# Operand rows of a trunk kernel at multiples of 64 bytes: wider rows of the normalised input and a padded scratch tile

## The chip, the core and the metric

The kernel runs on one core of a Trainium2 chip. The metric is the time of one execution on the device in microseconds, as the median of several runs. A profile of one more execution shows each instruction with its start and its duration, the DMAs, and the clock that TensorE was granted.

## What is computed

A trunk of two layers on 256 tokens with 1024 channels. Each layer is a SwiGLU FFN, a mixer (pooling in layer 0, a gated short convolution in layer 1) and a second FFN. Every sub-layer first normalises its input and modulates it by a shift and a scale, and a gate weighs what it adds; shift, scale and gate come from a vector c by one more product. A last normalisation ends it.

```python
D_MODEL, SEQ, DEPTH, D_FF = 1024, 256, 2, 2816
...
    cond = jax.nn.silu(c)
    for i in range(DEPTH):
        mod = (cond @ ada_w[i] + ada_b[i]).reshape(B, N_SUB, N_MOD, D_MODEL)
        shift, scale, gate = mod[:, :, 0], mod[:, :, 1], mod[:, :, 2]
        h = modulate(rms_norm(x, norm_g[i, 0]), shift[:, 0], scale[:, 0])
        x = x + 0.5 * gate[:, 0, None, :] * swiglu(h, ffn_w_in[i, 0], ffn_w_out[i, 0])
        h = modulate(rms_norm(x, norm_g[i, 1]), shift[:, 1], scale[:, 1])
        ...
        x = x + gate[:, 1, None, :] * y
        h = modulate(rms_norm(x, norm_g[i, 2]), shift[:, 2], scale[:, 2])
        x = x + 0.5 * gate[:, 2, None, :] * swiglu(h, ffn_w_in[i, 1], ffn_w_out[i, 1])
    return rms_norm(x, final_g)
```

## The kernel before

**Two parts for each number.** Most products are done three times over: a float32 number is split into a high part, rounded to the type float32r, and a low part, which is the rest, and the product is hi x hi + lo x hi + hi x lo. The helper mm3 (L135) issues these three matmuls. A matmul has 128x128 weights, loaded by an instruction of its own (LDWEIGHTS), and streams the other operand, 256 tokens wide as a rule; it adds to a bank of the result memory. The tokens stay resident.

**Weights.** They come from memory in units of 1 MB, 128 partitions with 2048 floats each, by DMAs that SyncE issues in the order of use. raw_unit (L191) takes one of four buffers raw. ScalarE copies raw to the high part hi (L230), and VectorE subtracts to get the low part lo (L237); hi and lo have four buffers each. A few units have their parts in gh and gl, the tiles of the FFN's inner values, while these are out of use: there gh and gl are weights, in the first block or two of an input product. The modulation's units go through raw too, with two dot products on VectorE each (L253). One product unit feeds 48 matmuls of 256 columns.

**Inputs.** hh and hl hold the high and the low part of the modulated input, a row of 256 tokens for each of eight blocks k of channels. hh's rows have two floats more, since the first blocks of an FFN begin before the normalisation is known, and carry the two parts of the shift as columns 256 and 257 (shift_columns, L374; mm3s, L380). hf is a float32 version of the same, for the products that use raw weights whole. The input products of the FFNs write banks f00b, f01b, f10b and f11b (and f01a, f10a, f11a for early blocks), in the loop

```python
700  for k in range(KB):
701      for s in range(2):
702          mm3(pab[:, s], (hi[:, k, s], lo[:, k, s]), h_pair(k), k == 0 and s == 0, k == KB - 1)
```

so that one block is 8 rows k with six matmuls each: 48. There are 22 blocks in an FFN: of f00 the first eight go together as the modulation comes in (seven of their eight rows in float32r), of f01, f10 and f11 the first three, two and three are early ones, and the convolution has six later blocks with 72 matmuls each (pcv and pb) behind two early ones (pe). The output products (out_product, L421) write accf and accc with gh and gl as the streamed operand. In the last product (out_last, L474) the roles are changed: gh and gl are the weights, and hi and lo are streamed, in pieces of 512 or 256 columns, to acco. In the pooling mixer, mean (L759) multiplies by mh, a matrix with the averaging windows on its diagonal and zeros elsewhere, as the streamed operand, with gh and gl as weights, to accp.

**Order.** The order on each engine is the order in the code, written out by hand (manual_schedule): low(n) and high(n) say how many units ahead the parts are made.

**Where the tiles lie.** A pool puts its tiles one behind the other, each rounded up to a multiple of 32 bytes in a partition. The pool "one" comes first, then "wk" for scratch, and then "wp" for the weights. In the memory map of the program before:

| tile | bytes in a partition | start, modulo 64 | its rows start at |
|---|---|---|---|
| hf | 8 x 1028 | 32 | 32 + 4k |
| gh, gl | 22 x 1024 | 0 | 0 |
| hh | 8 x 1032 | 0 | 8k |
| hl | 8 x 1024 | 0 | 0 |
| mh | 8256 | 0 | 0 |
| ss (three buffers, the last of wk) | 8, with 32 set aside | 0, 32, 0 | |
| raw, hi, lo (twelve buffers) | 8192 | 32 | 32 |

The weights of one matmul are 128 floats, 512 bytes, so all within a unit have the unit's place. The lines that the text speaks of:

```python
132  def mm(dst, w, m, start, stop):
133      PE.matmul(dst, w, m, start=start, stop=stop, skip_group_check=True)
...
339  hh = one.tile([P, KB, T + 2], F32R, name="hh")
340  hl = one.tile([P, KB, T], F32R, name="hl")
...
382      mm(dst, w[0], hh[:, k], k == 0, False)
383      mm(dst, w[1], hh[:, k], False, False)
384      mm(dst[:, :T], w[0], hl[:, k], False, k == KB - 1)
...
508              s = wk.tile([P, 2], F32, tag="ss", name=f"ss{b}{i}", bufs=3)
```

Of the kernel before, what the change touches and what calls it, by code (L numbers as in the profile page):

```python
# [9 lines left out]
F32 = mybir.dt.float32  # L10
F32R = mybir.dt.float32r
# [14 lines left out]
EDGE = 16  # L26
BAND = P + EDGE
# [15 lines left out]
class Source:  # L43
    """Cuts the weights into [128, 2048] units."""
# [45 lines left out]
def products():  # L90
    """The weight units of the products, in the order of their use. With each, the first of eight
    blocks of the products' inputs that hold its parts, where those are out of use by then; or,
    where it is used whole, whose buffer holds it: that of a high or of a low part."""

    def ffn(layer, f, at, first=False):
        into = [("ffn_first", layer, f, kb) for kb in range(KB)] if first else []
        into += [("ffn_in", layer, f, c) for c in range(0 if into == [] else NFIRST, FC)]
        out = [(("ffn_out", layer, f, u), None) for u in range(FC // 2)]
        return [(c, at[i] if i < len(at) else None) for i, c in enumerate(into)] + out

    conv = []
    for j in range(KB):
        conv.append((("conv_cv", j), 0 if j == 0 else None))
        if j % 2 == 0:
            conv.append((("conv_b", j // 2), 8 if j in (0, 4) else None))
    conv += [(("conv_out", u), None) for u in range(KB // 2)]
    first = ffn(0, 0, WHOLE, True)
    return (
        first[:-TAIL] + [(("pool",), "hi")] + first[-TAIL:]
        + ffn(0, 1, ("hi", "lo", "lo")) + ffn(1, 0, (0, 8)) + conv + ffn(1, 1, (8,))  # L110
    )
# [3 lines left out]
def trunk(ctx: ExitStack, tc: tile.TileContext, calls, consts: bass.AP, c_in: bass.AP,  # L115
# [19 lines left out]
    def mm3(dst, w, m, start, stop):  # L135
        """dst += w.T @ m; w, m: pairs of parts."""
        mm(dst, w[0], m[0], start, False)
        mm(dst, w[1], m[0], False, False)
        mm(dst, w[0], m[1], False, stop)

# [15 lines left out]
    # Token t to token v, for each window: the causal mean, less the token itself. From its place  # L156
    # on the diagonal a token's weights span BAND tokens; those of the first tokens, whose windows
    # are cut, come in with the constants, for a mean over the whole window: cut_means() makes it
    # that over the tokens there are.
# [15 lines left out]
    def table(func):  # L175
        """Has the function's table on the engine before it is needed."""
        tabs.append(wk.tile([P, 1], F32, tag="tab", name=f"tab{len(tabs)}"))
        S.activation(tabs[-1], eps, func)

    # Around the pooling mixer: after which blocks of the FFN's fed input one of its later block's  # L180
    # products goes; how many modulation units go with the blocks of the product before, into the
    # mixer, and with the pairs of blocks after; how far ahead the low parts are then.
# [43 lines left out]
    def high(n, parts=1):  # L226
        """The high parts of the products' next n units."""
        for _, raw, hi, _ in next_of("hi", n):
            for at in spans(parts) if hi else ():
                S.copy(hi[:, at], raw[:, at])  # L230

    def low(n, parts=1):
        """The low parts of the products' next n units."""
        high(n, parts)
        for _, raw, hi, lo in next_of("lo", n):
            for at in spans(parts) if hi else ():
                V.tensor_sub(lo[:, at], raw[:, at], hi[:, at].bitcast(F32))  # L237
# [11 lines left out]
    mods = {}  # L249

    def dot(out, w, init):
        """out = init + sum over w * cond; w becomes w * cond."""
        V.tensor_tensor_reduce(w, w, cond, 1.0, init, ALU.mult, ALU.add, out)  # L253

    def mod_dots(layer, sub, mod, w, lo):
        """Blocks lo... of one modulation vector, with what its use adds to it."""
        key, n = (layer, sub, mod), w.shape[1]
        if key not in mods:
            mods[key] = one.tile([P, KB], F32, name=f"mod{layer}{sub}{mod}")
        b = ada_col(layer, sub, mod) + lo  # L260
        for i in range(n):
            dot(mods[key][:, lo + i : lo + i + 1], w[:, i], cst[:, b + i : b + i + 1])
        mod_finish(key, lo, n)
# [24 lines left out]
    def spread(keys, lo, hi, later=0):  # L288
        """Spreads modulation vectors, but for the last parts, over the slots lo...hi of the
        stream of products to come."""  # L290
        ada_todo.extend((*k, q) for k in keys for q in range(4))
        slots.clear()
        n = len(ada_todo) - later
        for i in range(n):
            at = lo + (i * (hi - lo)) // n
            slots[at] = slots.get(at, 0) + 1
# [31 lines left out]
    def rstd_by_token(name):  # L328
        """With the tokens on the partitions: [128, 2]."""
        m = bank(f"ms{name}")  # L330
        for b in range(2):
            PE.matmul(m[:, 0, b : b + 1], sqs["a"][:, b * P : (b + 1) * P], ones[:, 0:1], start=True, stop=True)
        r = wk.tile([P, 2], F32, tag="rt", name=f"rt{name}", bufs=2)
        S.activation(r, m[:, 0, :2], AF.Sqrt, bias=eps)
        q = wk.tile([P, 2], F32, tag="rt", name=f"rq{name}", bufs=2)
        V.reciprocal(q, r)
        return q

    hh = one.tile([P, KB, T + 2], F32R, name="hh")
    hl = one.tile([P, KB, T], F32R, name="hl")  # L340

    def modulated(layer, sub, k, rstd, to):
        """x * rstd * g * (1 + scale) + shift: its high part, or all of it, and what makes the low
        one."""
        scale, shift = (mods[layer, sub, m][:, k : k + 1] for m in (SCALE, SHIFT))
        t = wk.tile([P, T], F32, tag="t", name=f"t{layer}{sub}{k}", bufs=4)
        V.scalar_tensor_tensor(t, x[:, k], scale, rstd, ALU.mult, ALU.mult)
        S.activation(to[:, k, :T], t, AF.Identity, bias=shift)
        return lambda: V.scalar_tensor_tensor(
            hl[:, k], t, shift, hh[:, k, :T].bitcast(F32), ALU.add, ALU.subtract  # L350
        )
# [13 lines left out]
    def scaled(layer, sub, k, to):  # L365
        """x * g * (1 + scale): what modulated() gives, before rstd and the shift."""
        sc = mods[layer, sub, SCALE][:, k : k + 1]
        S.activation(to[:, k, :T], x[:, k], AF.Copy, scale=sc)
# [5 lines left out]
    def shift_columns(layer, sub, ks=slice(0, KB)):  # L374
        """The shift's two parts beside scaled(), so that the product carries them too."""
# [4 lines left out]
    def mm3s(dst, w, k):  # L380
        """dst += w.T @ [scaled | shift's parts]"""
        mm(dst, w[0], hh[:, k], k == 0, False)
        mm(dst, w[1], hh[:, k], False, False)
        mm(dst[:, :T], w[0], hl[:, k], False, k == KB - 1)

    def unscaled(acc, rstd, name, split=True):
        """The product with the modulated input, in two parts: acc * rstd and the shift's."""
# [33 lines left out]
    def out_product(kind, n, layer, sub, name, after, first_slot, ahead, ready, between=lambda b: None, before=lambda u: None, whole=False):  # L421
        """x += gate * (z @ w), z: n blocks of parts, w: n // 2 units."""
# [39 lines left out]
    def by_token(a, b):  # L462
        """Of the residual and of its gate: channels 32 a..., for tokens 32 b...: tokens on the
        partitions."""
# [9 lines left out]
    def out_last(n, ahead):  # L474
# [24 lines left out]
        for b in range(2):  # L499
            mean, late = eps, []  # L500
            for i, (lo, hi) in enumerate(PIECES[b]):
# [6 lines left out]
                s = wk.tile([P, 2], F32, tag="ss", name=f"ss{b}{i}", bufs=3)  # L508
# [61 lines left out]
    def ffn_start(rstd, name):  # L570
        """The first blocks of the first FFN: all of them at once, as the modulation comes in."""
# [52 lines left out]
    def ffn_early(layer, f, sub, name, groups):  # L624
        """The first blocks of an FFN, begun before rstd is known."""
# [20 lines left out]
    def ffn_fed(layer, f, sub, name, feed, n, ahead):  # L646
        """The same where the input, used whole, comes two blocks at a time: the n-th block fills
        the time between."""
# [83 lines left out]
    def pool_shift():  # L732
        """The shift's product with the pooling mixer's weights, the same for each token."""
# [12 lines left out]
    def pool_layer(after, each):  # L746
# [12 lines left out]
        def mean(acc, g, z, at, first, last):  # L759
            """acc += the means, less the token itself, of the tokens' z."""  # L760
# [158 lines left out]
def blocks(a):  # L919
    """[..., 1024] to [128, ... * 8]: the channel within its block first."""  # L920
# [4 lines left out]
def edge():  # L925
    """For the first tokens: token t to token v, with the weight of a whole window, less the token
    itself as often as its own window holds it; and whole windows over their own."""
# [39 lines left out]
```

## Time and profile before

| | |
|---|---|
| median of three runs | 900.67 us (900.6 to 901.98) |
| span of the profiled execution, first to last instruction | 899.1 us |
| median less span | 1.6 us |
| TensorE busy | 881.2 us, 98% |
| VectorE busy | 717.1 us, 80% |
| ScalarE busy | 419.1 us, 47% |
| matmuls | 6972 |
| DMA | 235.59 MB, 262 GB/s over the span |

The profiled execution has no time of its own beside its span; the runs' median lies 1.6 us above the span. PE stands for TensorE's matmuls, PEld for its weight loads, DVE for VectorE, ACT for ScalarE, SP for SyncE. Matmuls are pipelined: the duration of one is longer than the time to the start of the next, and busy time counts overlapping ones once.

### The profile page before, as it was taken

The page shows a single profiled execution, that of the slowest core. Times are in us where ns is not written, and L with a number is a line of the kernel's source. Part 1 is how long each engine was busy: PE and PEld are TensorE (multiplying, and loading weights), DVE is VectorE, ACT ScalarE, POOL GpSimd, SP SyncE. Part 2 cuts the span into 40 slices and gives each one's busy share as a digit, 9 for nine tenths or more (in the row PEclk, how much of TensorE's full clock was granted, in tenths as well). Part 3 has the DMA queues.
Part 4 walks back from the last instruction along what each step waited for, and adds up shares of the span by engine and source line. Part 5 has one row for each costly group of instructions (what it writes and reads, how often), then busy time and mean ns, then how long its engine had stood idle before and what let it go on. Part 6 is the DMA issues. An engine that isn't in the chain of part 4 may idle for free.

```text
span 899.1 us, 16410 instructions
## 1 busy us (share of the span) xinstructions
PE 881.2 (98%) x6972; PEld 862.4 (96%) x6972; DVE 717.1 (80%) x1020; ACT 419.1 (47%) x544; POOL 7.5 (1%) x24
## 2 busy tenths in 40 slices
PE   4999999999999999999999999999999999999997
PEld 2999999999899999999999999999999999999886
DVE  6989998847889977868888988859877789754774
ACT  5454544424655444446644444336444755444432
POOL 3000000000000000000000000000000000000000
PEclk9999999999999999999999999999999999999999
DMA  8898899778649988886389989973364539855501
GB/s 346 326 343 328 317 376 354 286 279 329 214 161 332 362 294 300 315 317 234 99 299 335 354 314 327 381 280 142 141 232 149 207 121 347 290 183 183 197 38 47
DMA packets 33338, 235.59 MB, mean 262 GB/s; under 512 B 3697, under 2 KB 3825, under 8 KB 4978
## 3 DMA queue, kind: packets, MB, share of 16 engines
q1 hardware_dynamic: 33266, 234.56, 70.5%
q8 instruction: 54, 0.88, 0.4%
q14 instruction: 18, 0.15, 0.0%
HBM read 233.49 MB, written 1.05 MB: 261 GB/s over the span
## 4 chain that ended last, share of the span: by engine, by line
PE 97%; DVE 1%; DMA 1%; ACT 1%; issue 0%; SPq 0%; ACTq 0%
PE accf L133 21%; PE f00b L133 14%; PE f10b L133 13%; PE f01b L133 13%; PE f11b L133 13%; PE acco L133 7%; PE pcv L133 4%; PE accc L133 3%; PE pe L133 2%; PE pb L133 2%; PE f01a L133 1%; PE f11a L133 1%; PE f10a L133 1%; PE accz L133 1%; DVE raw L253 1%; DMA x<-xt 1%
## 5 line engine op out<-in xcount | busy, mean ns | idle before, releaser
L237 DVE TENSOR_TENSOR lo<-raw,hi 128x2048 fp32r<-128x2048 f32 (+1 forms) x137 | 298.7, 2192 | 38.9 <-ACT hi L230 38.8
L230 ACT CAST hi<-raw 128x2048 fp32r<-128x2048 f32 (+1 forms) x151 | 263.0, 1756 | 129.3 <-PE accf L133 42.6
L253 DVE CUSTOM_DVE_ANT_0 raw<-raw,cond,cst 128x1024 f32<-128x1024 f32 x144 | 179.4, 1278 | 14.9 <-DMA raw<-wall 14.5
L133 PE MATMUL accf<-gh,hi 128*128 128x256 f32 x528 | 149.6, 283 | 0.0
L133 PE MATMUL accf<-gh,lo 128*128 128x256 f32 x528 | 149.1, 282 | 0.0
L133 PE MATMUL accf<-gl,hi 128*128 128x256 f32 x528 | 148.1, 280 | 0.0
L133 PEld LDWEIGHTS accf<-gl,hi 128*128 128x128 f32 x528 | 100.4, 190 | 0.0
L133 PEld LDWEIGHTS accf<-gh,lo 128*128 128x128 f32 x528 | 99.2, 188 | 0.0
L133 PEld LDWEIGHTS accf<-gh,hi 128*128 128x128 f32 x528 | 98.8, 187 | 0.0
L133 PE MATMUL f00b<-hh,lo 128*128 128x256 f32 x336 | 94.9, 282 | 0.0
L133 PE MATMUL f00b<-hh,hi 128*128 128x256 f32 x336 | 94.8, 282 | 0.0
L133 PE MATMUL f00b<-hl,hi 128*128 128x256 f32 x336 | 94.5, 281 | 0.0
L133 PE MATMUL f10b<-hh,lo 128*128 128x256 f32 x320 | 90.3, 282 | 0.0
L133 PE MATMUL f11b<-hh,lo 128*128 128x256 f32 (+1 forms) x320 | 90.3, 282 | 0.0
L133 PE MATMUL f10b<-hh,hi 128*128 128x256 f32 x320 | 90.3, 282 | 0.0
L133 PE MATMUL f11b<-hh,hi 128*128 128x256 f32 (+1 forms) x320 | 90.3, 282 | 0.0
L133 PE MATMUL f10b<-hl,hi 128*128 128x256 f32 x320 | 90.2, 282 | 0.0
L133 PE MATMUL f11b<-hl,hi 128*128 128x256 f32 x320 | 90.2, 282 | 0.0
L133 PE MATMUL f01b<-hl,hi 128*128 128x256 f32 x304 | 86.2, 284 | 0.0
L133 PE MATMUL f01b<-hh,hi 128*128 128x256 f32 x304 | 85.9, 283 | 0.0
L133 PE MATMUL f01b<-hh,lo 128*128 128x256 f32 x304 | 85.8, 282 | 0.0
L133 PEld LDWEIGHTS f00b<-hh,lo 128*128 128x128 f32 x336 | 63.6, 189 | 0.2
(235 smaller groups left out, 1887.7 us busy)
## 6 DMA issues: line engine op xcount, KB each, us to landing
raw<-wall SPq DMA_DIRECT2D x221, 1024.0 KB, 5.3
x<-xt SPq DMA_DIRECT2D x4, 256.0 KB, 4.0
out<-x SPq DMA_DIRECT2D x4, 256.0 KB, 2.1
rows<-fg SPq DMA_DIRECT2D x1, 512.0 KB, 8.0
cst<-consts SPq DMA_DIRECT2D x1, 176.0 KB, 4.7
cond<-cvec SPq DMA_DIRECT2D x1, 4.0 KB
```

Source lines behind the costliest of these rows:

```text
L133: PE.matmul(dst, w, m, start=start, stop=stop, skip_group_check=True)
L230: S.copy(hi[:, at], raw[:, at])
L237: V.tensor_sub(lo[:, at], raw[:, at], hi[:, at].bitcast(F32))
L253: V.tensor_tensor_reduce(w, w, cond, 1.0, init, ALU.mult, ALU.add, out)
```

## The change

The row of hh is widened from 258 to 272 floats, and the scratch tile ss from 2 to 16. mm3s, which took whole rows of hh, now names the 258 columns. All else in the difference is comments and texts that describe functions.

```diff
+LINE = 16
...
-    hh = one.tile([P, KB, T + 2], F32R, name="hh")
+    hh = one.tile([P, KB, T + LINE], F32R, name="hh")
     hl = one.tile([P, KB, T], F32R, name="hl")
...
-        mm(dst, w[0], hh[:, k], k == 0, False)
-        mm(dst, w[1], hh[:, k], False, False)
+        mm(dst, w[0], hh[:, k, : T + 2], k == 0, False)
+        mm(dst, w[1], hh[:, k, : T + 2], False, False)
         mm(dst[:, :T], w[0], hl[:, k], False, k == KB - 1)
...
-                s = wk.tile([P, 2], F32, tag="ss", name=f"ss{b}{i}", bufs=3)
+                s = wk.tile([P, LINE], F32, tag="ss", name=f"ss{b}{i}", bufs=3)
```

## Rows read from the trace of the kernel before

**Rows 1.** The page: engines' busy time, share, instructions; chain that ended last.
```profile
span 899.1 us, 16410 instructions
...
PE 881.2 (98%) x6972; PEld 862.4 (96%) x6972; DVE 717.1 (80%) x1020; ACT 419.1 (47%) x544; POOL 7.5 (1%) x24
...
PE 97%; DVE 1%; DMA 1%; ACT 1%; issue 0%; SPq 0%; ACTq 0%
```

**Rows 2.** Groups of instructions: busy us, mean ns of one, idle before.
```profile
L133 PE MATMUL accf<-gl,hi 128*128 128x256 f32 x528 | 148.1, 280 | 0.0
```

**Rows 3.** One tile's instructions: ns min/median/max, first and last start (accf: 358.9 to 422.35).
```profile
L133 PE MATMUL accf<-gh,hi x176: 279/281/285, 359.1 to 422.1; 128*128 128x256 f32 x176
...
L133 PE MATMUL f10b<-hh,hi x320: 276/282/287, 434.2 to 548.6; 128*128 128x256 f32 x160
```

**Rows 4.** Timeline, TensorE: one block of f10b, first matmul of each k: start, us.
```profile
485.86 0.28 PE L133 MATMUL f10b<-hh,hi 128*128 128x256 f32 x1
...
486.57 0.29 PE L133 MATMUL f10b<-hh,hi 128*128 128x256 f32 x1
...
487.30 0.28 PE L133 MATMUL f10b<-hh,hi 128*128 128x256 f32 x1
...
488.01 0.28 PE L133 MATMUL f10b<-hh,hi 128*128 128x256 f32 x1
...
488.73 0.28 PE L133 MATMUL f10b<-hh,hi 128*128 128x256 f32 x1
...
489.45 0.28 PE L133 MATMUL f10b<-hh,hi 128*128 128x256 f32 x1
...
490.18 0.28 PE L133 MATMUL f10b<-hh,hi 128*128 128x256 f32 x1
...
490.88 0.28 PE L133 MATMUL f10b<-hh,hi 128*128 128x256 f32 x1
...
491.59 0.28 PE L133 MATMUL f10b<-hh,hi 128*128 128x256 f32 x1
```

**Rows 5.** Timeline, TensorE: the pooling mixer's means, 50 matmuls apart.
```profile
221.76 0.28 PE L133 MATMUL accp<-mh,gh 128*128 128x256 f32 x1
...
227.43 0.28 PE L133 MATMUL accp<-mh,gh 128*128 128x256 f32 x1
```

**Rows 6.** Timeline, TensorE: last product, nine wide matmuls, then six narrow ones.
```profile
844.81 0.40 PE L133 MATMUL acco<-hi,gh 128*128 128x512 f32 x1
...
846.92 0.28 PE L133 MATMUL acco<-hi,gh 128*128 128x256 f32 x1
...
847.63 0.40 PE L133 MATMUL acco<-hi,gh 128*128 128x512 f32 x1
```

**Rows 7.** Timeline, TensorE: early blocks with gh, gl as weights; k = 0, 1, 6.
```profile
422.44 0.28 PE L133 MATMUL f10a<-hh,gh 128*128 128x258 f32 x1
...
423.15 0.28 PE L133 MATMUL f10a<-hh,gh 128*128 128x258 f32 x1
...
426.71 0.28 PE L133 MATMUL f10a<-hh,gh 128*128 128x258 f32 x1
```

**Rows 8.** Stretches: length, engines' busy us, granted clock, DMA share, GB/s.
```profile
30.00:150.00 120.00, 120.00 (x1008) 119.87 (x1007) 110.76 (x160) 60.76 (x79) 0.00 (x0) 1.00 0.93 346
...
255.00:330.00 75.00, 75.00 (x630) 75.00 (x630) 67.33 (x100) 36.85 (x46) 0.00 (x0) 1.00 0.82 297
...
420.00:555.00 135.00, 135.00 (x1131) 134.94 (x1130) 115.72 (x171) 66.06 (x89) 0.00 (x0) 1.00 0.74 268
...
570.00:585.00 15.00, 15.00 (x127) 15.00 (x126) 13.17 (x15) 5.14 (x3) 0.00 (x0) 1.00 0.99 387
```

**Rows 9.** VectorE, lines L349 and L237: ns min/median/max, first and last start.
```profile
L349 DVE SCALAR_TENSOR_TENSOR hl<-t,mod,hh x39: 474/480/487, 20.1 to 724.1; 128x256 fp32r<-128x256 f32 x39
...
L237 DVE TENSOR_TENSOR lo<-raw,hi x137: 1215/2284/2295, 60.5 to 872.3; 128x2048 fp32r<-128x2048 f32 x125, 128x1024 fp32r<-128x1024 f32 x12
L237 DVE TENSOR_TENSOR gl<-raw,gh x6: 2284/2286/2293, 403.8 to 691.2; 128x2048 fp32r<-128x2048 f32 x6
```

## The prediction

> **What bounds the kernel now.** I read the page first: TensorE is busy for 881.2 of 899.1 us and makes up 97% of the chain that ended last, VectorE is second with 80% [rows 1]. A busy TensorE is not yet a TensorE at its peak, because its matmuls overlap: a row says 280 ns for one matmul, but the next starts after about 120 ns [rows 2, 3]. What sets the time is therefore the pitch, from one start to the next, times the number of matmuls. So I read starts, not durations.
>
> In the output product of one FFN the 176 triples of accf start between 359.1 and 422.1 us: 63.0 / (175 x 3) = 120.0 ns a matmul. In the input product of the next FFN 320 triples of f10b start between 434.2 and 548.6 us: 114.4 / (319 x 3) = 119.5 ns [rows 3]. Neither has gaps. [...] So a change that doesn't take out matmuls can only help here through the pitch.
>
> **Whether the start of an operand moves the pitch.** Four groups of rows bear on it. The matmuls compared are all 128x128 weights with float32r operands.
>
> First, one block of f10b, with hi and lo at 32 bytes past a multiple of 64, and the rows of hh at 8k bytes past one for row k. Its eight steps of six matmuls last .71, .73, .71, .72, .72, .73, .70 and .71 us [rows 4]. Rows 1, 3 and 5 are the slow ones (mean .727), the even rows have .710, and row 7 has .71. So the start of a row is worth some 2 ns a matmul.
>
> Second, accp in the pooling mixer, the only long run of 256 columns in which both operands (mh, and gh or gl as weights) start at multiples of 64: 50 matmuls from 221.76 to 227.43 us, 113.4 ns [rows 5]. Against accf, where the weights alone are off by 32, that is 6.6 ns less, for the same columns.
>
> Third, the last product: weights gh and gl at multiples of 64, streamed hi and lo at 32. Nine matmuls of 512 columns take 2.11 us, 234.4 ns each, and six of 256 take .71 us, 118.3 ns [rows 6]. The wide ones run above twice accp's pitch (226.8 ns), although each of them has the same 128 columns of weights to load as a narrow one: what is lost goes with the columns streamed.
>
> Fourth, against it: f10a and f10b's first blocks have weights in gh and gl, at multiples of 64. Their 36 matmuls from 422.44 to 426.71 us have 118.6 ns, and row 0 of hh, where everything lies at a multiple of 64, needs .71 us for six, no less [rows 7]. But two of three there stream 258 columns, which end 8 bytes into the next line. No row shows 256 columns with all of it aligned but accp, and accp also differs in its order (one streamed row, two weights). I take the price nearer accp, because it alone has the form and the alignment which the changed matmuls get.
>
> **The change part by part.** hh's rows grow from 258 to 272 floats: 1032 to 1088 bytes, 17 x 64, so every row starts at a multiple of 64. The tile grows by 8 x 56 = 448 bytes, 7 x 64, so hl, up, mh and the scratch behind it keep their place within 64. ss grows from 8 to 64 bytes a buffer, of which 32 were set aside: three buffers add 96 bytes. raw, hi and lo, which follow, move by 544 bytes, from 32 to 0 modulo 64. No instruction, DMA or wait is added or taken out, and mm3s still streams 258 columns. The DMAs into raw keep their form and land 544 bytes higher; no row shows them at another start, and I take nothing, with the stretches where their share is near 1 as the place of a loss. hf stays as it is, so its float32 products are no part of the sum, and "all operands" holds for the float32r ones.
>
> The terms, with accp's 113.4 ns as the new pitch:
> - Output products: accf 3 x 528 and accc 192 (4 units x 48) make 1776. They save 120.0 - 113.4 = 6.6 ns each: 11.7 us [rows 2, 3, 5].
> - Input products with 256 columns: 14 + 19 + 20 + 19 blocks of 48, 336 for the first eight blocks, and 6 x 72 in the convolution, 4224 in all. They save 119.5 - 113.4 = 6.1 ns: 25.8 us.
> - Last product: 198 with 512 columns, 234.4 - 226.8 = 7.6 ns: 1.5 us; 132 with 256 columns, 4.9 ns: .6 us [rows 6].
> - The 384 of the early blocks, with 258 columns and their partners: nothing, since rows 7 show none; at most 5.2 ns, 2.0 us.
> - accp itself: nothing, it has its alignment before and after.
>
> Together 39.6 us. The other engines' instructions move too. I cost that at nothing, from both sides: hl is made from rows of hh at all eight offsets in 474 to 487 ns, and the split of a unit takes 2284 to 2293 ns into gl, whose operand gh is aligned, as against 2284 (median) into lo, from hi at 32 [rows 9]. A loss there would have VectorE's slack as cover, and that is the part that can fail.
>
> **What the faster TensorE runs into.** From 30 to 150 us VectorE is busy for 110.8 of 120 us and the DMA share is .93 at 346 GB/s [rows 8]. At the new pitch TensorE needs 120 x 113.4 / 119.4 = 114.0 us. VectorE would have to be busy 97% of it and the DMAs to bring 364 GB/s; the best row shows 387. It works out on average, but VectorE takes work in order, and a late low part holds TensorE. I take half of the 6 us of that stretch as lost. From 255 to 330 us VectorE's 67.3 us would face 71.2, 95%; I take 1.5 of 3.8 us as lost. Elsewhere its share stays under 91% (420 to 555 us: 115.7 of then 128.2), and I take nothing. So 39.6 - 4.5 = 35 us.
>
> **Sum.** The profiled span is 899.1 us; the runs' median of 900.7 lies 1.6 above it. 899.1 - 35 + 1.6 = 865.7, say 866 us. Bounds of this case: without the loss and with the early blocks 39.6 + 2.0 = 41.6, 859 us, and 857 if the wide matmuls save more than twice what a narrow one does; if only half of the pitch is given back, 881 us. Its own range is 857 to 881.
>
> **Rivals.**
> - Only part of a line counts. What rows 4 show for certain is that odd rows of hh cost (.727 - .710) / 6 = 2.8 ns more in rows 1, 3 and 5; with row 7 the four odd ones exceed the even by 2.1 ns. Half of 4224 would save that: 2112 x 2.1 = 4.4 us, and the move of the weights, already at a multiple of 16, nothing: 896 us. For it speaks that the even offsets (0, 16, 32, 48) hardly differ; against it that accf, with rows of gh all at 0, has 120.0 and not 118.
> [...]
> - The starts don't set the pitch at all: accp is fast by its order of operands. Rows 7 speak for it. Then nothing moves: 899 to 902 us.
> - Slower. The cost could lie in the two streams of TensorE starting in the same phase, not in either being off. Before, weights at 32 and rows at 8k meet in changing phases; after, all share one. The aligned first step of rows 7 is no faster than the rest, and accf, in one phase all along, is slower than f10b by .5 ns. If all 4224 go to accf's pitch the price is 2.1 us, 903 us; if they go to that of the worst step of rows 4, .73 / 6 = 121.7 ns, it is 9.3 us, 910 us. It decides as soon as the mean pitch exceeds 119.9 ns. Against it: accp, with both operands in one phase, is the fastest run there is.
> - VectorE or the DMAs become the bound. At its limit in 30 to 330 us, where nothing at all would be saved, some 15 of the 39.6 us (300 x 6.0 / 119.4) are gone: 876 us, within the forecast's own range.
>
> **How the numbers follow.** Chances: forecast .58, part of a line .14, no effect .16, slower .12. A difference under .2% (1.8 us) can't be told from none in this kernel. Faster by more is .58 + .14 = .72, within it .16, slower .12. The range must leave out no more than 2 in 10: below 857 I leave .03, at the top the slower case (.12) and the upper edge of "no effect" (.04). So it reaches from 857 to 901.5, while the likeliest case keeps 857 to 881.
>
> **What would show it.** Right: accf's triples and f10b's start every 340 ns instead of 360 and 358; the steps of a block are equal, without slow odd rows; the wide matmuls of acco come near 227 ns; accp keeps 113.4; VectorE's durations stay, its share rises to 83%, and gaps before TensorE matmuls appear between 30 and 150 us, with low parts as releaser. Part of a line: equal steps of .71 in f10b, with accf still at 120.0. No effect: all pitches as before. Slower: f10b at 120 ns or more in every step. The forecast is wrong if accp's pitch comes from its order, from its streamed rows, which are mostly zeros, or from its place in memory above 64 bytes; none of these can be told from the trace of before.

## The result and the profile after

The changed kernel takes 890.98 us (890.41 to 891.83) against 900.95 beside it: a ratio of 0.989, interval 0.987 to 0.990. It is faster by 10 us, where I had forecast 35. The stated range of 857 to 901.5 us held the time, but only because it was stretched for the rivals; the likeliest case's 857 to 881 did not. The size, and the cause that it was worked out from, were wrong.

The page of the changed kernel, its span and engines:
```profile
span 889.7 us, 16410 instructions
...
PE 871.6 (98%) x6972; PEld 852.9 (96%) x6972; DVE 717.0 (81%) x1020; ACT 419.7 (47%) x544; POOL 8.0 (1%) x24
```
The span fell by 9.4 us, TensorE's busy time by 9.6; VectorE works as long as before [rows 1]. So the gain lies in TensorE's pitch, as the prediction had it. How much, the instructions of two tiles show, with first and last start (accf from 354.5 to 417 us):
```profile
L134 PE MATMUL accf<-gh,hi x174: 279/279/279, 355.6 to 416.8; 128*128 128x256 f32 x174
...
L134 PE MATMUL f10b<-hh,hi x320: 276/279/290, 429.7 to 542.7; 128*128 128x256 f32 x160
```
accf has 61.2 / (173 x 3) = 117.9 ns a matmul (117.8 from the starts to the nanosecond), f10b 113.0 / (319 x 3) = 118.1. Before they had 120.0 and 119.5 [rows 3]; accp's 113.4 [rows 5] did not come. And accp itself, which the change doesn't touch, lost it. In its timeline these two starts are 42 matmuls apart:
```profile
219.76 0.28 PE L134 MATMUL accp<-mh,gh 128*128 128x256 f32 x1
...
224.75 0.28 PE L134 MATMUL accp<-mh,gh 128*128 128x256 f32 x1
```
4.99 / 42 = 118.8 ns (118.6 over all its starts). mh and its weights gh and gl start at multiples of 64 as before; only mh has moved, by 448 bytes. This row alone contradicts the theory of the forecast. It also answers two other doubts of the prediction: accp's order of operands and its streamed zeros are the same in both kernels, so neither is what gave the 113.4 ns.

A block of f10b, first matmul of each row k, answers to [rows 4]:
```profile
480.75 0.28 PE L134 MATMUL f10b<-hh,hi 128*128 128x256 f32 x1
...
481.45 0.28 PE L134 MATMUL f10b<-hh,hi 128*128 128x256 f32 x1
...
482.15 0.28 PE L134 MATMUL f10b<-hh,hi 128*128 128x256 f32 x1
...
482.86 0.28 PE L134 MATMUL f10b<-hh,hi 128*128 128x256 f32 x1
...
483.58 0.28 PE L134 MATMUL f10b<-hh,hi 128*128 128x256 f32 x1
...
484.29 0.28 PE L134 MATMUL f10b<-hh,hi 128*128 128x256 f32 x1
...
484.99 0.28 PE L134 MATMUL f10b<-hh,hi 128*128 128x256 f32 x1
...
485.69 0.28 PE L134 MATMUL f10b<-hh,hi 128*128 128x256 f32 x1
...
486.41 0.28 PE L134 MATMUL f10b<-hh,hi 128*128 128x256 f32 x1
```
The steps are .70, .70, .71, .72, .71, .70, .70 and .72 us. They are not equal, though every row now starts at a multiple of 64, and they repeat after four rows (706, 698, 707 and 722 ns, twice, in all later blocks). Rows are 1088 bytes apart, so four rows are 4352 bytes, 17 x 256: these steps point to a period of 256 bytes, not 64.

### The profile page after: what moved, and what is told of

Its sections match the earlier page's. It is cut to its first block, busy times and chain, and to the rows that moved or that the text cites. A ratio compares the mean times of both kernels' runs of the same rounds, so it can differ in the third digit from the quotient of the medians.

```text
span 889.7 us, 16410 instructions
## 1 busy us (share of the span) xinstructions
PE 871.6 (98%) x6972; PEld 852.9 (96%) x6972; DVE 717.0 (81%) x1020; ACT 419.7 (47%) x544; POOL 8.0 (1%) x24
## 4 chain that ended last, share of the span: by engine, by line
PE 88%; DVE 6%; DMA 4%; ACT 1%; issue 1%; SPq 0%; ACTq 0%
PE accf L134 21%; PE f10b L134 13%; PE f01b L134 13%; PE f11b L134 13%; PE acco L134 7%; PE f00b L134 4%; PE pcv L134 4%; DMA raw<-wall 3%; DVE raw L254 3%; PE accc L134 3%; PE pe L134 2%; PE pb L134 2%; DVE lo L238 1%; PE f01a L134 1%; PE f11a L134 1%; PE accp L134 1%
## 5 line engine op out<-in xcount | busy, mean ns | idle before, releaser
L254 DVE CUSTOM_DVE_ANT_0 raw<-raw,cond,cst 128x1024 f32<-128x1024 f32 x144 | 179.5, 1280 | 12.5 <-DMA raw<-wall 12.2
L134 PE MATMUL accf<-gh,hi 128*128 128x256 f32 x528 | 147.5, 279 | 0.0
L134 PEld LDWEIGHTS f00b<-hh,hi 128*128 128x128 f32 x336 | 63.4, 189 | 0.0
```

## The experiments

**The theory.** From these rows I formed one that looks at the *distance*: where the streamed row starts, less where the weights start, modulo 256 bytes. In the memory maps, modulo 256, gh and gl start at 64 in both kernels, mh at 0 before and 192 after, hi and lo at 224 before and 0 after. So accp (mh streamed past gh and gl) had distance 192 before and 128 after, accf (gh and gl streamed past hi and lo) 96 before and 64 after. Its rivals: multiples of 64 count after all, or accp's order of operands does. The first step was to measure the pitch by itself.

```python
for i in range(60):   # w: start of the weights, m: start of the rows, in bytes
    a, b = w // 4 + 128 * (i % 8), m // 4 + 1024 * (i // 12 % 3)
    PE.matmul(acc[:, :n], wide[:, a : a + 128], rows[:, b : b + n], ...)
```


> Leaves out the whole trunk: it measures the pitch of 128x128 weights with streamed rows, in float32r, and its output is not the reference's. Runs of 60 matmuls; in each the weights start at w and the streamed rows at m, w and m counted from two places that are equal modulo 256 bytes. The distance m - w goes from 0 to 256 bytes in steps of 16 with 256 columns (tiles a0 to a256), then w at 64 with distances 0, 64, 128 and 192 (b64 to b256), then 512 columns in steps of 32 (c), then 258 columns in steps of 64 (e). Theory of distances: the pitch follows the distance from weights to rows modulo 256 bytes, which in the main kernel's traces was 192 for the means before the change (113.4 ns), 128 for them after it (118.6), 96 for accf before (120.0) and 64 after (117.8). It expects about 113.4 ns in a192, near 118 in a64 and a128, 120 or more in a0 and a256, and b equal to a at the same distance. Theory of multiples of 64: a0, a64, a128, a192 and a256 alike, the steps between them slower by 2 ns or more. Theory of the order of operands: no tile differs from another by over 1 ns.

The timeline of this bench, 40 matmuls in the middle of a run each, at distances 64, 96, 112, 128, 160, 192 and 256 (that is 0) in this order; columns are the first start, the time to the last end, and the tile:
```profile
53.03 4.87 PE L43 MATMUL a<-rows,weights 128*128 128x256 f32 x40
...
67.33 4.96 PE L43 MATMUL a<-rows,weights 128*128 128x256 f32 x40
...
74.43 4.70 PE L43 MATMUL a<-rows,weights 128*128 128x256 f32 x40
...
81.30 4.91 PE L43 MATMUL a<-rows,weights 128*128 128x256 f32 x40
...
95.52 4.86 PE L43 MATMUL a<-rows,weights 128*128 128x256 f32 x40
...
109.67 4.70 PE L43 MATMUL a<-rows,weights 128*128 128x256 f32 x40
...
137.83 4.96 PE L43 MATMUL a<-rows,weights 128*128 128x256 f32 x40
```
Less the last one's .28 us, over 39 pitches: 117.7, 120.0, 113.3, 118.7, 117.4, 113.3 and 120.0 ns. Two distances of sixteen are fast, 192 and, unexpected, 112; the others have 116.7 to 120.0. Distances 0 and 256 agree, as a period of 256 bytes asks. Runs b, with the weights 64 bytes further, give the same as a (120.0, 117.8, 118.7, 113.3). 512 columns need 226.7 ns at distance 0, 229 at 64 and 233 to 234 elsewhere; 258 columns 119 to 122 at all four distances tried, in line with the early blocks, which showed nothing [rows 7]. The bench has the main kernel's pitches, with hardly any work of other engines in it (in its span of 317.4 us ScalarE is busy for 8.6, VectorE for .9 and GpSimd for .2):

| | distance | main kernel, ns | bench, ns |
|---|---|---|---|
| accf before | 96 | 120.0 | 120.0 |
| accf after | 64 | 117.8 | 117.8 |
| accp before | 192 | 113.4 | 113.3 |
| accp after | 128 | 118.6 | 118.7 |

The agreement is for rows that all lie at one distance. In f10b of the changed kernel the distance of hh's rows goes through 64, 128, 192 and 0, with hl at 64; by the bench's pitches the four steps would be 707, 710, 689 and 716 ns, and they are 706, 698, 707 and 722. For mixed distances the theory gives no forecast.

The edits of the kernels below are shown against the changed kernel, the times against the kernel before, run beside each.

**The weights' part of the change alone.**
```diff
-    hh = one.tile([P, KB, T + LINE], F32R, name="hh")
+    hh = one.tile([P, KB, T + 2], F32R, name="hh")
```


> One part of the change: the scratch tile is padded (raw, hi and lo at multiples of 64 bytes), hh keeps rows of 258 floats. hi and lo then lie 64 bytes past a multiple of 256, as gh does: distance 0 for accf. Theory of multiples of 64: accf has both operands at multiples of 64, so it goes to the 117.8 ns of the changed kernel, and the kernel is faster than before by 4 to 8 us. Theory of distances: accf at distance 0 is at 120 ns or above, not faster than before, and the kernel is within 3 us of before or slower; the means keep their 113.4 ns, since their distance stays 192.

898.33 us against 900.96, ratio 0.997 (0.996 to 0.998). accf stays at 120.0 ns, although both its operands now start at multiples of 64, at distance 0. accp keeps 113.3. Most of what is gained comes from the input products (118.9 ns on average), and .8 us from the last product, whose wide matmuls go from 233.8 to 229.3 ns: they now lie at distance 0, in the bench the best one for 512 columns (226.7 there).

**The rows' part alone.**
```diff
-                s = wk.tile([P, LINE], F32, tag="ss", name=f"ss{b}{i}", bufs=3)
+                s = wk.tile([P, 2], F32, tag="ss", name=f"ss{b}{i}", bufs=3)
```


> The other part of the change alone: hh's rows of 272 floats, the scratch tile unpadded, so that hi and lo stay 32 bytes past a multiple of 64 (160 modulo 256 here), distance 160 to gh and hl. Theory of distances: accf at the 117.3 ns that distance 160 showed in the bench, against 120.0 before, 4.8 us less; the input products lose their dependence on the row of hh in steps of 8 bytes and repeat after four rows; the kernel between 888 and 896 us, so most of the gain comes without the weights at multiples of 64. Theory of multiples of 64: accf stays at 120.0, the input products gain 1.3 ns at most, 895 us or more.

891.82 us against 901.52, ratio 0.990 (0.988 to 0.991): nearly the whole gain of the change, with every weight of hi and lo 32 bytes off a multiple of 64. accf has 117.3 ns, near the 117.4 that the bench gives at distance 160; f10b has 118.1. One number doesn't fit: accp has 120.0 ns here and 118.6 in the changed kernel, with mh, gh and gl at the same places, distance 128. So the distance doesn't always fix the pitch; why not here stays open.

**The changed kernel with the weights 64 and 128 bytes further.** All starts stay at multiples of 64.
```diff
-                s = wk.tile([P, LINE], F32, tag="ss", name=f"ss{b}{i}", bufs=3)
+                s = wk.tile([P, LINE], F32, tag="ss", name=f"ss{b}{i}", bufs=4)   # 5 for 128 bytes
```


> The changed kernel with one more buffer of the padded scratch tile, so that raw, hi and lo lie 64 bytes further on; every start stays at a multiple of 64. Distance from hi and lo to gh 0 in place of 64. Theory of multiples of 64: nothing changes, accf 117.8 ns, 891 us. Theory of distances: accf at 120 ns or more (it saw 127 ns in single matmuls of the changed kernel where hh's row is at distance 0), the kernel slower than the changed one by 4 us or more.

> The changed kernel with two more buffers of the padded scratch tile: raw, hi and lo 128 bytes further on, every start at a multiple of 64, distance to gh and hl 192. Theory of multiples of 64: nothing changes, 891 us. Theory of distances: accf and accc fall from 117.8 to about 113.4 ns, 1776 x 4.4 = 7.8 us less; the input products, whose rows of hh lie at all four distances while hl is at 192, gain on the third of their matmuls that stream hl and stay about as they are on the others, 0 to 10 us less; 873 to 883 us.

64 bytes: 896.69 us (ratio 0.995 to before, 0.993 to 0.997), accf at 120.0. 128 bytes: 886.25 us (0.984, 0.982 to 0.987), which the theory had at 873 to 883; it missed. In the second kernel accf shows why, in the output products of f01 and f10:
```profile
L134 PE MATMUL accf<-gh,hi x176: 276/276/281, 354.2 to 413.7; 128*128 128x256 f32 x176
...
L134 PE MATMUL accf<-gh,hi x173: 281/281/281, 539.1 to 599.9; 128*128 128x256 f32 x173
```
The same code at the same distance has 59.5 / 525 = 113.3 ns in the one and 60.8 / (172 x 3) = 117.8 in the other. A pitch can have two steady states. The input products, too, gained less than the theory allowed: f10b has 117.8 ns.

**The same distance after different leads.** Runs of 60 at distance 192 (g) and 112 (h), each after 24 matmuls of another kind.

> Leaves out the whole trunk; its output is not the reference's. Runs of 60 matmuls with 256 columns at distance 192 (tiles g) and then at distance 112 (tiles h), the two distances that gave 113.3 ns before, each after a lead of 24 matmuls: at distances 0, 32, 64, 96, 128, 160, 224, 192 and 112, then with 258 columns, with 12 float32 matmuls, and with 512 columns. It asks why accf at distance 192 ran at 113.3 ns in two FFNs and at 117.8 ns in the third and in the convolution of the kernel with the weights 128 bytes further. Theory of history: the pitch at one distance has more than one steady state, and the matmuls before decide which; some g runs stay at 117.8 ns over all 60 matmuls, others are at 113.3. Theory of distance alone: all g runs settle at 113.3 within 20 matmuls, and the difference in the main kernel comes from something else, such as other engines' accesses or which buffer is read.

The middle of three runs: distance 192 after a lead at 64 and after one at 128, distance 112 after one at 128:
```profile
46.35 4.81 PE L40 MATMUL gk<-rows,weights 128*128 128x256 f32 x41
...
65.75 4.87 PE L40 MATMUL gm<-rows,weights 128*128 128x256 f32 x40
...
187.90 4.58 PE L40 MATMUL hm<-rows,weights 128*128 128x256 f32 x39
```
113.3, 117.7 and 113.2 ns. At 192 four leads of twelve (128, 160, float32, 512 columns) leave the run at 117.8 ns to its last matmul, the other eight end at 113.3. At 112 all twelve settle at 113.3. The lead's distance alone doesn't decide: in the first bench a run at 192 followed 60 matmuls at 128 and had 113.3. Each bench ran once, so whether the same lead always brings the same state isn't shown; nor were the other fourteen distances tried after many leads.

**All streamed rows at one distance.** hh's rows get 1280 bytes, 5 x 256, so they no longer differ; the weights are placed by buffers of the scratch tile.
```diff
-    hh = one.tile([P, KB, T + LINE], F32R, name="hh")
+    hh = one.tile([P, KB, T + 64], F32R, name="hh")
...
-        weight = wk.tile([P, 2, BAND], F32, name=f"mw{g}", tag="mw")
+        weight = wk.tile([P, 2, BAND], F32, name=f"mw{g}", tag="mw", bufs=1)
...
-                s = wk.tile([P, LINE], F32, tag="ss", name=f"ss{b}{i}", bufs=3)
+                s = wk.tile([P, LINE], F32, tag="ss", name=f"ss{b}{i}", bufs=6)   # distance 0; 7 for 192
```


> The same with raw, hi and lo 64 bytes lower: every streamed row at distance 0 from the weights, all starts at multiples of 64 as in the changed kernel. Theory of distances: 120.0 ns in accf and in the input products alike, about 900 us, no gain against before though every operand is at a multiple of 64. Theory of multiples of 64: 891 us as in the changed kernel.

> hh's rows 1280 bytes long (320 floats, a multiple of 256), and raw, hi and lo placed so that every streamed row of hh, hl, gh and gl lies 192 bytes past the weights modulo 256. To make room one scratch buffer of the mixer's setup is dropped. Theory of distances: accf, accc and the input products fall to 113.4 ns where they find the fast state; with all of them 6000 x 4.6 = 27 us less than the changed kernel, 864 us, less what VectorE holds back; with half of them in the slow state of 117.8 ns, 877 us. Theory of multiples of 64: no change against 891 us.

Distance 0: 903.47 us, ratio 1.003 (1.001 to 1.004), slower than before, with every operand of these products at a multiple of 64. Its f10b and accc, over 957 and 189 matmuls:
```profile
L134 PE MATMUL f10b<-hh,hi x320: 278/283/283, 435.8 to 550.6; 128*128 128x256 f32 x160
...
L134 PE MATMUL accc<-gh,hi x64: 283/283/283, 683.9 to 706.5; 128*128 128x256 f32 x64
```
120.0 and 119.6 ns (120.0 from the starts to the nanosecond). That ends the theory of multiples of 64. Distance 192: 880.94 us, ratio 0.980 (0.974 to 0.987), somewhat more than the 864 to 877 expected; but its four executions have 876.37, 877.63, 884.25 and 888.88, far more scatter than any other kernel. In the profiled one (877.63) f00, f01 and their output products run at 113.3 ns, f10, f11 and accc at 117.8: two states again. In the convolution one can see the pitch change over. Its first two later blocks, then its last two:
```profile
L134 PE MATMUL pcv<-hh,hi x32: 276/276/280, 610.9 to 626.5; 128*128 128x256 f32 x32
...
L134 PE MATMUL pcv<-hh,hi x32: 281/281/281, 644.2 to 660.5; 128*128 128x256 f32 x32
```
There are 138 matmuls from the first start to the last in either row: 113.4 and 117.8 ns (starts to the nanosecond), at the same distance. Between them lie two blocks in which pb has its weights in gh and gl, so at another distance. That the scatter is the states' share in each execution is likely, but only one of the four has a trace.

**Distance 112, at no multiple of 64.**
```diff
-    gh = one.tile([P, FC, T], F32R, name="gh")
+    def shifted(n, row, name):
+        t = one.tile([P, n * row + 64], F32R, name=name)
+        return t[:, 4 : 4 + n * row].rearrange("p (n t) -> p n t", n=n)
+
+    gh = shifted(FC, T, "gh")   # gl, hl alike; hh = shifted(KB, T + 64, "hh")
...
-        weight = wk.tile([P, 2, BAND], F32, name=f"mw{g}", tag="mw")
+        weight = wk.tile([P, 2, BAND], F32, name=f"mw{g}", tag="sa")
...
-                s = wk.tile([P, LINE], F32, tag="ss", name=f"ss{b}{i}", bufs=3)
+                s = wk.tile([P, 8], F32, tag="ss", name=f"ss{b}{i}", bufs=5)
```


> hh's rows 1280 bytes long, and gh, gl, hh and hl 16 bytes past a multiple of 64 (80 modulo 256), hi and lo at 32 bytes past one (224 modulo 256): no streamed row and no weight of hi and lo starts at a multiple of 64, and every streamed row is 112 bytes past the weights modulo 256, the distance at which the bench came to 113.3 ns after every lead. Theory of distances with history: accf, accc, pcv and the input products with 256 columns at 113.3 ns in all stages and in every execution; 6000 x 4.6 = 27.6 us less than the changed kernel, 863 us if VectorE and the DMAs keep up, up to 870 if they hold TensorE back between 30 and 330 us; the scatter between executions of the kernel at distance 192 (876 to 889 us) is gone. Theory of multiples of 64: 900 us or more, as before the change. Theory that the gain needs both, the distance and the multiples of 64: 118 ns and above, 890 us or more.

868.13 us (867.25 to 870.73), ratio 0.964 (0.963 to 0.965): 32.7 us less than before, and better than both kernels. Page, the same two tiles, and one of the convolution:
```profile
span 867.4 us, 16411 instructions
...
PE 846.6 (98%) x6972; PEld 827.0 (95%) x6972; DVE 715.2 (82%) x1020; ACT 420.8 (49%) x544; POOL 7.7 (1%) x24
...
L134 PE MATMUL f10b<-hh,hi x320: 275/275/283, 419.7 to 528.2; 128*128 128x256 f32 x160
...
L134 PE MATMUL accc<-gh,hi x64: 275/275/275, 655.7 to 677.2; 128*128 128x256 f32 x64
...
L134 PE MATMUL pb<-hh,gh x16: 278/278/283, 623.0 to 639.0; 128*128 128x256 f32 x16
```
108.5 / 957 = 113.4 ns and 21.5 / 189 = 113.8 (113.3 from the starts). All output products and the FFNs' input products with 256 columns have this pitch, apart from gaps and the first matmuls of a stage; the wide scatter is gone (3.5 us over five executions). Some places stay slow, against what I expected of "all stages". In the convolution's blocks 4 and 5 pb has its weights in gh and gl, at distance 0 from hh, and pb and pcv alternate there; 135 matmuls from the first start of the row shown to its last give 16.0 / 135 = 118.5 ns, where the other four blocks settle at 113.3. The 258 columns of the early blocks have 118.5 to 120, the last product, at distance 144, has 233.9 and 118.5, and accp 120.0. And now TensorE waits for VectorE, as its waits between 30 and 330 us show (total us, times, longest):
```profile
PE f00b L134 <- DVE lo L616: 1.3, 1, 1.3
PE f00b L134 <- DVE lo L242: 0.9, 1, 0.9
PE f00b L134 <- DVE gf L553: 0.5, 1, 0.5
```
In the kernel of before no wait of TensorE for VectorE's low parts was listed.

**Start and width.** Distances 192, 112 and 0 with the weights at 0, 4, 16, 32 and 48 bytes, and weights of 64 and 32 columns.

> Leaves out the whole trunk; its output is not the reference's. Runs of 48 matmuls with 256 columns, weights of 128 columns starting at 0, 4, 16, 32 and 48 bytes (tiles i to m), rows at distance 192 (a), 112 (b) and 0 (c) from them, each after a lead of 24 at distance 112; then weights of 64 columns (h) and of 32 (q) at distances 0, 64, 96, 112, 128 and 192. Theory of distances: the pitch follows the distance whatever the start, 113.3 ns in a and b and 120 in c, at least for starts in steps of 16. Theory of multiples of 64: only starts at 0 reach 113.3. If the cost is a meeting of the two streams of reads, the one of the weights and the one of the rows, then with 64 and 32 columns of weights the differences between distances shrink to a half and a quarter, about 3 and 2 ns; if it is a property of the streamed rows alone, they stay at 4 to 7 ns.

| distance | start 0 | 4 | 16 | 32 | 48 | 64 columns | 32 columns |
|---|---|---|---|---|---|---|---|
| 192 | 113.3 | 121.1 | 113.3 | 113.3 | 113.3 | 119.2 | 113.3 |
| 112 | 113.3 | 121.3 | 120.0 | 113.3 | 120.0 | 116.7 | 113.3 |
| 0 | 120.0 | 122.3 | 118.3 | 120.0 | 118.3 | 113.3 | 117.8 |

(Mean pitch in ns over the last matmuls of each run. Start is that of the weights; the rows move with it. The last two columns have start 0 and no lead between the runs.) Distances hold for starts 32 bytes apart, not for all in steps of 16, so the theory was right in part: of the starts tried, 112 is fast only with the weights at 0 and 32. The kernel at distance 112 agrees: its accp has mh 112 bytes past gh and gl, which start 16 past a multiple of 64, and 120.0 ns. With narrower weights the differences don't shrink as a meeting of two streams of reads was expected to make them; from the fastest to the slowest they stay at 4 to 6 ns, and the order of the distances turns round (0 is fastest with 64 columns). So the number of the weights' columns changes which distance is good, and the cost is no property of the streamed row alone; what brings it about stays open.

## Why the prediction was wrong, point by point

- **What bounds the kernel, and that only the pitch counts: right.** All of the gain is in the starts of TensorE's matmuls.
- **The step that failed** is the choice between the second and the fourth group of rows: "I take the price nearer accp, because it alone has the form and the alignment which the changed matmuls get." accp's 113.4 ns were read as the price of starts at multiples of 64. The runs show they are the price of distance 192 between rows and weights, in the faster of its two states: accp lost them when mh moved by 448 bytes, accf at multiples of 64 has 113.3, 117.8 or 120.0 ns by its distance (at 192, either of the first two), and a kernel with all of it at multiples of 64 and at distance 0 is slower than before. The last paragraph of the prediction named this way to fail, "its place in memory above 64 bytes", as one that the trace couldn't tell. The memory map could have helped: mh's distance to gh differed from every other pair's.
- **The terms.** Output products: 6.6 ns expected, 120.0 - 117.8 = 2.2 measured, 1776 x 2.2 = 3.9 us in place of 11.7. Input products: 6.1 expected, 119.5 - 118.1 = 1.4 measured in f10b, less in others (pcv .7); summed over the starts of all their tiles 4.9 us in place of 25.8. Last product: about 1 ns on the wide ones and 2.6 on the narrow ones by their mean starts, .5 us in place of 2.1. accp, costed at nothing, loses 5.2 ns a matmul, but with the gaps around it takes 7.9 us before and after. Together 9.3; the span fell by 9.4. The gain is thus that of distances that happened to be better: 64 for 96 in accf, and for hh a mixture of four multiples of 64.
- **The rows against it, rows 7,** were right in what they said, that alignment alone brings nothing there, but not a clean case: with 258 columns the bench finds no fast distance among four.
- **Padding the scratch tile.** Its part alone brings 2.6 us, the rows' alone 9.7, both 10. The intervals are too wide to tell from these that the parts don't add up, but the tiles show it: f10b gains .6 ns by the one, 1.4 by the other and 1.4 by both, for each part sets distances for the other.
- **Other engines unmoved: right.** VectorE has 717.0 us, as before.
- **What a faster TensorE runs into** couldn't show in the change, but does at distance 112: the sum had 39.6 us less 4.5 lost, and that kernel gains 32.7. By the starts, the output products give 11.8 us (11.7 in the sum), the input products 19.3 (25.8), the last product nothing (2.1). Gaps in f00b between 30 and 150 us are listed as 2.7 us of waits, 2.2 of them for VectorE's low parts; f00b takes some 4 us more than its matmuls at 113.4 ns would. I had taken 3 as lost there, and 1.5 between 255 and 330 us, where no wait is listed.
- **Rivals.** "Part of a line" gave 896 us, nearer than the forecast, but not by its mechanism: the steps of a block are not equal (.70 to .72 us), and accf did not stay at 120.0 (117.8). It took the weights' move, from one multiple of 16 bytes to another, as worth nothing; the bench shows 113.3 to 120.0 ns among starts that are all multiples of 16, so these are not alike. "Same phase" would be distance 0, and that kernel's 903.5 us lie within the rival's 903 to 910. But distances 80 and 96 have 120.0 ns too, so it isn't the same phase as such that costs, and the change did not end up there.

In all, the runs show a pitch of equal matmuls that depends on where weights and rows lie to each other, by 6.7 ns of 113.3; through what, no run shows.

## What to carry to other kernels

Where float32r matmuls run back to back, read the pitch from starts, and compare it with where one operand starts less where the other does, modulo 256 bytes, not with alignment as such: here it went from 113.3 to 120.0 ns with the first, and was 120.0 with every operand at a multiple of 64 and at distance 0. A fast run that differs from the slow ones in two ways is a lead, not a price: measure the pitch over distances in a bench of its own, before laying out tiles by it, with the width and the weights' start of your own matmuls. Prefer a distance that settles at the fast pitch after every lead you try (112 did after twelve of twelve here, 192 after eight), and give rows a length that is a multiple of 256 bytes, as the 1280 of the kernel with 868.13 us, so that they share it.

## What the runs showed of the hardware that was not expected

- The pitch of 128x128 weights with 256 float32r columns, at a mean granted clock of .997 to .998 in the benches, lies between 113.3 and 120.0 ns by the distance of the operands modulo 256 bytes, with starts in steps of 16; with both operands 4 bytes off it is 121 to 122.
- At distance 192 there are two steady states, 113.3 and 117.8 ns; one lasted over 170 triples of matmuls, 61 us. In the bench they differed by what ran before, but what decides between them is open. accp at distance 128 had 118.6 in one kernel and 120.0 in another.
- 258 columns cost 119 to 122 ns, up to 9 ns more than 256 at the good distance: with the two columns of the shift the pitch is slow at all four distances tried, and 118 to 121 in the early blocks of every kernel here.
- 512 columns have their best distance, of the eight tried, at 0 (226.7 ns), one of the worst for 256 (120.0).
